# A fused LoRA kernel: ScalarE's spreads go into hardware loops, the casts to GpSimd, and the last loaded tile goes as 120 rows and 8

## The chip, the core and the metric

The kernel runs on one core of a Trainium2 chip. TensorE multiplies matrices, VectorE and ScalarE work element by element, GpSimd helps with copies, SyncE issues the transfers, and 16 DMA engines move the data between the chip's main memory and the core's own memory (SBUF). TensorE writes to PSUM.

The metric is the time of one execution on the device in microseconds (us). Three runs of the kernel before took 123.73, 123.73 and 123.92 us; the median is 123.73.

## The reference

```python
x: 16 x 512 x 768, A: 768 x 16, B: 16 x 768, all float32; scale = 0.5

def reference(x, A, B, scale):
    lora = np.matmul(np.matmul(x, A), B)
    return (x + scale * lora).astype(np.float32)
```

The output is as large as x, 25.17 MB each. Both go through the DMA engines once; A and B are small.

## The kernel before

**Tiles and parts.** x has 8192 rows of 768 numbers, 64 tiles of 128 rows. All 64 tiles have their own place in SBUF (`x_all`), and the result is added into the same place. `PARTS` cuts the 64 tiles into five parts of 8, 16, 16, 12 and 12; each partition holds neighbouring rows, so that one row of a transfer is long. Eight loads (`LOADS`) bring x in, five stores (`STORES`), one for each part, take the result out. All are issued by SyncE, in program order, on one queue.

**Groups.** The computation runs over 16 groups of four tiles (`GROUP`). A group g goes through these steps:

1. *cast* (`narrowed`, L221): four tiles of x, float32, become float16. ScalarE casts the first two tiles and GpSimd the other two.
2. *transpose* (`turned`, L277): VectorE transposes the cast group in 32 x 32 blocks into `xt`.
3. *project* (`projected`, L312): TensorE multiplies with `w_bd`, A laid out in blocks; 24 matmuls add up in PSUM (`ps_yt`).
4. *spread* (L263): ScalarE scales the product and writes it, by four instructions of 32 partitions, to the diagonal blocks of `y_bd`.
5. *raise* (`raised`, L333): TensorE multiplies with B into `lora_ps`, in two halves.
6. *add* (`summed`, L282): VectorE adds the two halves to x in place.

`xt`, the transposed group, exists once. `y_bd`, `ps_yt` and the halves of `lora_ps` exist twice. TensorE runs a hardware loop of eight rounds, each with two groups (L354): project g, raise g-1. The other engines' programs are written out at full length. VectorE's order is transpose g, then the two adds of group g-2.

**Where the cast group lies.** For groups 0 to 7 it lies in the last two of the tiles that the last load fills later (`xn_a`); for groups 8 to 10 (`PLACE`) in `xt` itself; from group 11 on in the first tiles of `x_all`, which the first store has emptied by then (`xn_c`). Each is one buffer, so the cast of a group waits until the group before it has been transposed (`s_taken`, an increment by the second matmul of each projection), in groups 8 to 10 until the projection before it is done (`s_y`), and group 11 waits for the first store (`s_out0`). VectorE's transpose waits for the projection before it, since it overwrites `xt`, and for both halves of its cast.

**SyncE's order.** The first two loads, A and B, four more loads; the seventh load once the setup's buffers in its place are free; then it waits for the adds of the first two parts and for eight projections to have begun, issues the last load, waits for the seventh load to land, and issues the stores of parts 0 and 1; the stores of parts 2 to 4 follow as their last adds finish.

**Setup.** GpSimd clears buffers, prepares `w_one` from A and copies it into three of the four diagonal blocks of `w_bd` (L247), waiting after each copy; VectorE makes the fourth copy (L292).

Of the kernel before, what the change touches and what calls it, by code (L numbers as in the profile page):

```python
# [16 lines left out]
GROUP = 4  # L17

SUB = 2
# [4 lines left out]
PLACE = range(8, 11)  # L24
# [7 lines left out]
def kernel(  # L32
# [10 lines left out]
    P = 128  # L43
# [50 lines left out]
        v = x_all[:, ds(t, SUB), :].rearrange("p s d -> p (s d)").bitcast(MM_DT)  # L94
        return v.rearrange("p (s d) -> p s d", s=GROUP)

    xn_a, xn_c = narrow_in(ROOM - SUB), narrow_in(0)

    def narrow_of(g):
        return xn_a if g < PLACE[0] else xt if g in PLACE else xn_c  # L100

    sems = []

    def sem(name):
        sems.append(nc.alloc_semaphore(name))
        return sems[-1]
# [22 lines left out]
    ]  # L129
    s_load = [sem(f"s_load{k}") for k in range(len(LOADS))]  # L130

    def load_of(t):
        i, s = where[t]
        return next(k for k, ld in enumerate(LOADS) if ld[0] == i and ld[1] <= s < ld[1] + ld[2])
# [9 lines left out]
    s_y, s_lora = sem("s_y"), sem("s_lora")  # L144
    s_spread = [sem(f"s_spread{h}") for h in range(2)]


# [13 lines left out]
    def on_sync(e):  # L161
        def load(k):
            ld = LOADS[k]
            e.dma_start(out=held(*ld), in_=memory(x2, *ld)).then_inc(s_load[k], 16)

        def summed(k):
            e.wait_ge(s_sum, k + 1)
            if STORED[k] + 1 < NG:

                e.sem_inc(s_free[STORED[k] % 2][PAIRS - 1], 1)  # L170

        def store(k, done):
            st = STORES[k]
            e.dma_start(out=memory(out2, *st), in_=held(*st)).then_inc(done, 16)
# [34 lines left out]
    def narrowed(e, copy, g, first, n=SUB):  # L209
        t = g * GROUP + first  # L210
        for k in dict.fromkeys(load_of(t + k) for k in range(n)):
            if (e, k) not in here:
                here.add((e, k))
                e.wait_ge(s_load[k], 16)
# [6 lines left out]
        ins = copy(out=narrow_of(g)[:, ds(first, n), :], in_=tiles(t, n))  # L221

        ins.then_inc(s_narrow[g % 2] if g else s_first if first else s_a, 1)

    def on_gpsimd(e):
        e.memset(a_rows[0:Q], 0.0).then_inc(s_ready, 1)  # L226
        e.memset(b_rows, 0.0).then_inc(s_brows, 1)
        e.memset(pick, 0.0).then_inc(s_pick, 1)
        e.memset(w_bd.rearrange("p c k m -> p (c k m)").bitcast(fp32), 0.0)  # L229
        e.memset(y_bd.rearrange("p h s m -> p (h s m)").bitcast(fp32), 0.0).then_inc(s_ready, 1)  # L230
        e.wait_ge(s_pick, 1)
        e.affine_select(
            out=pick, in_=pick, compare_op=mybir.AluOpType.not_equal, fill=1.0, base=0,
            pattern=[[0, NQ], [-APART, Q]], channel_multiplier=1,
        ).then_inc(s_pick, 1)
        narrowed(e, e.tensor_copy, 0, 0)
        e.wait_ge(s_pick, 2)
        e.wait_ge(s_b, 16)
        e.tensor_copy(out=b_half, in_=b_rows).then_inc(s_bh, 1)  # L239
        e.wait_ge(s_ready, 3)  # L240
        e.tensor_copy(  # L241
            out=w_one.rearrange("i (c e) k r -> i c e (k r)", c=SETS),
            in_=a_t[0:Q].rearrange("i k r (e c) -> i c e (k r)", c=SET)[:, 0:SETS, 0:SET, :],
        ).then_inc(s_w, 1)
        e.wait_ge(s_w, 1)
        for b in range(NQ - 1):
            e.tensor_copy(  # L247
                out=w_bd[ds(b * Q, Q), :, :, ds(b * Q, R)], in_=w_one
            ).then_inc(s_w, 1)
            e.wait_ge(s_w, b + 2)  # L250
        for g in range(1, NG):
            narrowed(e, e.tensor_copy, g, SUB)

    def on_scalar(e):
        narrowed(e, e.copy, 0, SUB)
        e.wait_ge(s_bp, 1)
        e.copy(out=b_mm, in_=lora[0][:, 0, :]).then_inc(s_bm, 1)  # L257
        narrowed(e, e.copy, 1, 0)
        for g in range(NG):
            e.wait_ge(s_y, g + 1)  # L260
            for b in range(NQ):
                q = ds(b * Q, Q)
                last = e.mul(out=y_bd[q, g % 2, :, q], in_=y_ps[g % 2][q, :, :], mul=sc)  # L263
            last.then_inc(s_spread[g % 2], 1)
            if g + 2 < NG:
                narrowed(e, e.copy, g + 2, 0)

    def on_vector(e):
        e.wait_ge(s_a, SETS * 16 + 1)
        e.transpose(  # L270
            out=a_t[0:Q].rearrange("i k r c -> i (k r) c"),
            in_=a_rows[0:Q].rearrange("c (i k r) -> c (k r) i", k=2, r=R),
        ).then_inc(s_ready, 1)

        def turned(g):
            ts = [v.bitcast(fp32) for v in (xt, narrow_of(g))]
            e.transpose(out=ts[0], in_=ts[1]).then_inc(s_turned[g % 2], 1)  # L277

        def summed(g, p):
            xs = tiles(g * GROUP + 2 * p, 2)  # L280
            e.wait_ge(s_lora, (g + 1) * PAIRS + p + 1)
            ins = e.tensor_tensor(out=xs, in0=xs, in1=lora[p % 2], op=mybir.AluOpType.add)  # L282
# [7 lines left out]
        b = NQ - 1  # L290
        e.wait_ge(s_w, 1)
        e.tensor_copy(  # L292
            out=w_bd[ds(b * Q, Q), :, :, ds(b * Q, R)], in_=w_one
        ).then_inc(s_wv, 1)
        for t in range(1, NG + 2):
            if t < NG:
                e.wait_ge(s_y, t)
                e.wait_ge(s_narrow[t % 2], 2 * ((t + 1) // 2))  # L298
                turned(t)
            if t > 1:  # L300
                for p in range(PAIRS):
                    summed(t - 2, p)

    def on_tensor(e):


        def projected(h):
            xv = xt.rearrange("p s (c j k) -> p s c j k", c=NC, k=2)
            e.wait_ge(s_turned[h], 1)
            for m in range(MMS):  # L310
                c, k = divmod(m, 2)
                mm = e.matmul(  # L312
                    y_ps[h], w_bd[:, c, k, :], xv[:, :, c, :, k],
                    start=(m == 0), stop=(m == MMS - 1),
                )
                if m == 0:
                    mm.then_inc(s_turned[h], -1)
                if m == 1:

                    mm.then_inc(s_taken, 1)  # L320
                if m == MMS - 1:
                    mm.then_inc(s_y, 1)

        def raised(h, p):
            if p == 0:
                e.wait_ge(s_spread[h], 1)
            free = s_free[1 - h][p]
# [12 lines left out]
            mms[-1].then_inc(s_lora, 1)  # L340
# [70 lines left out]
```

## Time and profile before

| what | value |
|---|---|
| median of three runs | 123.73 us |
| the profiled execution | 123.87 us |
| its span, first to last instruction | 122.1 us |
| DMA traffic in the span | 50.45 MB, mean 413 GB/s |
| share of the span that data packets took on 16 engines | 96.7% |
| VectorE busy | 82.8 us, 68% |
| TensorE busy (matmul, weight load) | 56.6 us, 37.0 us |
| ScalarE busy | 42.8 us, 35% |
| GpSimd busy | 30.7 us, 25% |
| instruction packets in the span (queue 14) | 2, 0.02 MB |

The profile shows one execution. PE is TensorE's matmul, PEld its weight load, DVE is VectorE, ACT is ScalarE, POOL is GpSimd, SP is SyncE, and a q behind an engine's name means its sequencer, which issues transfers. "L277" is line 277 of the kernel before. The rows of DMA and GB/s cut the span into 40 slices (a digit is the busy share in tenths, 9 is 90% or more). A row of a group reads: line, engine, operation, output<-input with shapes, count | busy us, mean ns of one | idle time before it and what ended that. A row of the timeline reads: start in us, duration in us, engine, line, operation, count, and in brackets the idle time of the engine before it and what ended it. The DMA view can be asked for any stretch of the span; it counts the packets that start in it, how many of them are small, and what share of 16 engines' time over that stretch they took, by queue: q1 carries data, q14 instructions. A packet is counted with its whole duration where it starts, so a short stretch can show more than 100%.

### The profile page before, as it was taken

How to read it: one execution, taken by the hardware profiler on the slowest of the kernel's cores; microseconds unless marked ns; L12 is line 12 of the kernel's file. 1: busy time of each engine (PE TensorE's matmuls, PEld its weight loads, DVE VectorE, ACT ScalarE, POOL GpSimd, SP SyncE). 2: the span in 40 equal slices, each digit the busy share in tenths (PEclk: the TensorE clock that was granted, in tenths of full speed). 3: DMA queues.
4: the chain of work that ended last, by engine and by line, in shares of the span. 5: the costliest groups of instructions: out<-in, count | busy, mean ns of one | idle time of the engine just before them, and what ended most of it. 6: DMA issues, size and time to landing. Idle time of an engine off the chain costs nothing.

```text
span 122.1 us, 1371 instructions
## 1 busy us (share of the span) xinstructions
PE 56.6 (46%) x522; PEld 37.0 (30%) x522; DVE 82.8 (68%) x50; ACT 42.8 (35%) x82; POOL 30.7 (25%) x31
## 2 busy tenths in 40 slices
PE   0000278775764766737694608876475740000000
PEld 0000075453351542514464208444154320000000
DVE  0002905599999999999969649999999998000000
ACT  4003344782652735265252084474380300000000
POOL 7722660441340422224040044034040000000000
PEclk9999999999999999999859995899999999655555
DMA  3999999998998989999999999799799799899980
GB/s 60 421 441 439 443 419 435 435 548 370 403 515 379 459 387 399 439 395 427 431 431 467 430 499 467 322 515 467 306 515 483 305 495 423 387 423 507 423 387 36
DMA packets 1930, 50.45 MB, mean 413 GB/s; under 512 B 236, under 2 KB 236, under 8 KB 392
## 3 DMA queue, kind: packets, MB, share of 16 engines
q1 hardware_dynamic: 1928, 50.43, 96.7%
q14 instruction: 2, 0.02, 0.0%
HBM read 25.26 MB, written 25.17 MB: 413 GB/s over the span
## 4 chain that ended last, share of the span: by engine, by line
DMA 45%; DVE 25%; issue 5%; PE 4%; POOL 4%; SPq 1%; POOLq 0%; DVEq 0%
DMA x_sb<-in_x_dram 29%; DVE x_sb L282 15%; DMA out_dram<-x_sb 9%; DVE xt L277 9%; DMA x_sb<-in_A_dram 6%; PE ps_yt L312 3%; DVE x_sb L270 2%; POOL w_bd L247 1%; POOL x_sb L221 1%; SPq L181 1%; POOL x_sb L226 1%; POOL x_sb L241 1%; PE lora_ps L333 1%; POOLq L406 0%; DVEq L298 0%
## 5 line engine op out<-in xcount | busy, mean ns | idle before, releaser
L282 DVE TENSOR_TENSOR x_sb<-x_sb,lora_ps 128x1536 f32<-128x1536 f32 x32 | 54.0, 1730 | 0.0
L312 PE MATMUL ps_yt<-xt,w_bd 128*128 128x128 f16 x384 | 27.8, 233 | 19.7 <-DVE xt L277 17.0
L333 PE MATMUL lora_ps<-b_mm,y_bd 128*128 128x512 f16 (+1 forms) x136 | 28.7, 340 | 12.2 <-DVE x_sb L282 8.6
L312 PEld LDWEIGHTS ps_yt<-xt,w_bd 128*128 128x128 f16 x384 | 25.2, 103 | 25.7 <-issue 25.7
L221 ACT CAST x_sb<-x_sb 128x1536 f16<-128x1536 f32 x13 | 19.1, 1472 | 35.9 <-PE ps_yt L312 18.9
L221 POOL CAST x_sb<-x_sb 128x1536 f16<-128x1536 f32 x13 | 19.1, 1468 | 40.3 <-PE ps_yt L312 29.2
L277 DVE STREAM_TRANSPOSE xt<-x_sb 128x1536 f32<-128x1536 f32 x13 | 22.9, 1763 | 8.3 <-POOL x_sb L221 4.8
L333 PEld LDWEIGHTS lora_ps<-b_mm,y_bd 128*128 128x128 f16 x136 | 11.8, 102 | 25.3 <-DVE x_sb L282 11.7
L263 ACT ACTIVATE y_bd<-ps_yt 32x128 f16<-32x128 f32 x64 | 17.2, 268 | 6.2 <-PE ps_yt L312 5.3
L270 DVE STREAM_TRANSPOSE x_sb<-x_sb 32x1024 f32<-32x1024 f32 x1 | 1.9, 1941 | 11.3 <-DMA x_sb<-in_A_dram 11.3
L221 ACT CAST xt<-x_sb 128x1536 f16<-128x1536 f32 x3 | 4.4, 1472 | 9.6 <-PE ps_yt L312 9.6
L221 POOL CAST xt<-x_sb 128x1536 f16<-128x1536 f32 x3 | 4.4, 1469 | 13.0 <-PE ps_yt L312 13.0
L345 PE MATMUL lora_ps<-x_sb 128*128 128x512 f16 (+1 forms) x2 | 0.8, 500 | 12.6 <-POOL x_sb L239 12.6
L277 DVE STREAM_TRANSPOSE xt<-xt 128x1536 f32<-128x1536 f32 x3 | 5.3, 1778 | 1.1 <-POOL xt L221 1.0
L345 PEld LDWEIGHTS lora_ps<-x_sb 128*128 128x128 f16 x2 | 0.1, 104 | 12.5 <-issue 12.5
L239 POOL CAST x_sb<-x_sb 128x768 f16<-128x768 f32 x1 | 0.8, 829 | 4.6 <-DMA x_sb<-in_B_dram 4.6
L221 ACT ACT_TABLE_LOAD x1 | 1.3, 1283 | 0.9 <-SPq L159 0.9
L247 POOL COPY w_bd<-x_sb 32x384 f16<-32x384 f16 x3 | 1.5, 501 | 0.2
L229 POOL MEMSET w_bd<- 128x1536 f32 x1 | 1.4, 1373 | 0.0
L257 ACT CAST b_mm<-lora_ps 128x768 f16<-128x768 f32 x1 | 0.8, 799 | 0.8 <-PE lora_ps L345 0.8
L226 POOL MEMSET x_sb<- 32x1024 f32 x1 | 0.9, 942 | 0.5 <-SPq L159 0.5
L241 POOL CAST x_sb<-x_sb 32x384 f16<-32x384 f32 x1 | 0.8, 829 | 0.9 <-DVE x_sb L270 0.9
(9 smaller groups left out, 2.6 us busy)
## 6 DMA issues: line engine op xcount, KB each, us to landing
out_dram<-x_sb SPq DMA_DIRECT2D x2, 6144.0 KB, 24.0
x_sb<-in_x_dram SPq DMA_DIRECT2D x3, 3072.0 KB, 20.7
out_dram<-x_sb SPq DMA_DIRECT2D x2, 4608.0 KB, 18.0
x_sb<-in_x_dram SPq DMA_DIRECT2D x1, 6144.0 KB, 34.8
x_sb<-in_x_dram SPq DMA_DIRECT2D x1, 4608.0 KB, 45.2
out_dram<-x_sb SPq DMA_DIRECT2D x1, 3072.0 KB, 11.4
x_sb<-in_x_dram SPq DMA_DIRECT2D x1, 2304.0 KB, 9.6
x_sb<-in_x_dram SPq DMA_DIRECT2D x1, 1536.0 KB, 9.5
```

Source lines behind the costliest of these rows:

```text
L181: e.dma_start(out=a_rows[c : SET * SET : SET, :], in_=blocks[ds(c * SET, SET), :]).then_inc(s_a, 16)
L221: ins = copy(out=narrow_of(g)[:, ds(first, n), :], in_=tiles(t, n))
L226: e.memset(a_rows[0:Q], 0.0).then_inc(s_ready, 1)
L229: e.memset(w_bd.rearrange("p c k m -> p (c k m)").bitcast(fp32), 0.0)
L241: e.tensor_copy(out=w_one.rearrange("i (c e) k r -> i c e (k r)", c=SETS), in_=a_t[0:Q].rearrange("i k r (e c) -> i c e (k r)", c=SET)[:, ...
L247: e.tensor_copy(out=w_bd[ds(b * Q, Q), :, :, ds(b * Q, R)], in_=w_one).then_inc(s_w, 1)
L263: last = e.mul(out=y_bd[q, g % 2, :, q], in_=y_ps[g % 2][q, :, :], mul=sc)
L270: e.transpose(out=a_t[0:Q].rearrange("i k r c -> i (k r) c"), in_=a_rows[0:Q].rearrange("c (i k r) -> c (k r) i", k=2, r=R),).then_inc(s_r ...
L277: e.transpose(out=ts[0], in_=ts[1]).then_inc(s_turned[g % 2], 1)
L282: ins = e.tensor_tensor(out=xs, in0=xs, in1=lora[p % 2], op=mybir.AluOpType.add)
L312: mm = e.matmul(y_ps[h], w_bd[:, c, k, :], xv[:, :, c, :, k], start=(m == 0), stop=(m == MMS - 1),)
L333: mms.append(e.matmul(t[:, k, ds(n0, w)], y_bd[:, h, 2 * p + k, :], b_mm[:, ds(n0, w)], start=True, stop=True,))
```

## The change

- *Casts.* GpSimd now casts all four tiles of a group in one instruction, except in groups 8 to 10, where ScalarE and GpSimd still share. `xn_a` and `xn_c` become two buffers each, used in turn, so that a cast waits for the transpose of the group two before (`s_taken` at g-1). In groups 8 to 10 the cast waits for `s_raise`, an increment of the first matmul of each raise, where it waited for `s_y`.
- *Spreads.* ScalarE's spreads of groups 0 to 5 and of groups 10 to 15 stand in two hardware loops of three rounds with two spreads each; those of groups 6 to 9 are written out. In loops the counts that a wait is for can't grow, so `s_y` becomes one semaphore for each of the two buffers, set to one by the projection and taken back by the second instruction of the spread.
- *Waits of VectorE.* The transpose no longer waits for `s_y`; the third instruction of the spread of the group before counts into `s_narrow`, the semaphore of the casts, and the transpose waits for one number.
- *Setup.* The fourth copy into `w_bd` moves from VectorE to ScalarE. GpSimd no longer waits after each of its three copies, but once behind them.
- *The last load.* Its four tiles go as three transfers: three tiles over 128 partitions, then the fourth tile as 120 partitions and as 8. They count into one semaphore (48 in all).

```diff
-    xn_a, xn_c = narrow_in(ROOM - SUB), narrow_in(0)
+    xn_a = [narrow_in(ROOM - GROUP + SUB * h) for h in range(2)]
+    xn_c = [narrow_in(SUB * h) for h in range(2)]
...
+    MANY = 120
+
+    def load_pieces(ld):
+        i, s, n = ld
+        if ld is not LOADS[-1]:
+            return [(held(*ld), memory(x2, *ld))]
+        three, one = (i, s, n - 1), (i, s + n - 1, 1)
+        return [(held(*three), memory(x2, *three))] + [
+            (held(*one)[rows], memory(x2, *one)[rows]) for rows in (ds(0, MANY), ds(MANY, P - MANY))
+        ]
...
-            e.dma_start(out=held(*ld), in_=memory(x2, *ld)).then_inc(s_load[k], 16)
+            for to, of in load_pieces(ld):
+                e.dma_start(out=to, in_=of).then_inc(s_load[k], 16)
...
         if g in PLACE:
-            e.wait_ge(s_y, g)
+            e.wait_ge(s_raise, g)
         elif g == PLACE[-1] + 1:
             e.wait_ge(s_out0, 16)
-        elif g:
-            e.wait_ge(s_taken, g)
+        elif g > 1:
+            e.wait_ge(s_taken, g - 1)
...
-            e.wait_ge(s_w, b + 2)
+        e.wait_ge(s_w, NQ)
         for g in range(1, NG):
-            narrowed(e, e.tensor_copy, g, SUB)
+            if g in PLACE:
+                narrowed(e, e.tensor_copy, g, SUB)
+            else:
+                narrowed(e, e.tensor_copy, g, 0, GROUP)
...
-        narrowed(e, e.copy, 1, 0)
-        for g in range(NG):
-            e.wait_ge(s_y, g + 1)
+        b = NQ - 1
+        e.wait_ge(s_w, 1)
+        e.copy(out=w_bd[ds(b * Q, Q), :, :, ds(b * Q, R)], in_=w_one).then_inc(s_wv, 1)
+
+        def spread(h):
+            e.wait_ge(s_y[h], 1)
             for b in range(NQ):
                 q = ds(b * Q, Q)
-                last = e.mul(out=y_bd[q, g % 2, :, q], in_=y_ps[g % 2][q, :, :], mul=sc)
-            last.then_inc(s_spread[g % 2], 1)
-            if g + 2 < NG:
-                narrowed(e, e.copy, g + 2, 0)
+                ins = e.mul(out=y_bd[q, h, :, q], in_=y_ps[h][q, :, :], mul=sc)
+                if b == 1:
+                    ins.then_inc(s_y[h], -1)
+                if b == 2:
+
+                    ins.then_inc(s_narrow[1 - h], 1)
+            ins.then_inc(s_spread[h], 1)
+
+        def rounds(n):
+            with e.Fori(0, n):
+                for h in range(2):
+                    spread(h)
+
+        rounds(PLACE[0] // 2 - 1)
+        spread(0)
+        for g in PLACE:
+            narrowed(e, e.copy, g, 0)
+            spread((g - 1) % 2)
+        rounds((NG - PLACE[-1]) // 2)
...
+        count = [0, 0]
         for t in range(1, NG + 2):
             if t < NG:
-                e.wait_ge(s_y, t)
-                e.wait_ge(s_narrow[t % 2], 2 * ((t + 1) // 2))
+                count[t % 2] += 3 if t in PLACE else 2
+                e.wait_ge(s_narrow[t % 2], count[t % 2])
                 turned(t)
...
                 if m == MMS - 1:
-                    mm.then_inc(s_y, 1)
+                    mm.then_inc(s_y[h], 1)
...
             if p == 0:
+                mms[0].then_inc(s_raise, 1)
                 mms[2].then_inc(s_spread[h], -1)
```

More of the change, by code (lines that the diff above doesn't have):

```diff
@@ L95, in narrow_in @@
         return v.rearrange("p (s d) -> p s d", s=GROUP)
-    xn_a, xn_c = narrow_in(ROOM - SUB), narrow_in(0)
+    xn_a = [narrow_in(ROOM - GROUP + SUB * h) for h in range(2)]
+    xn_c = [narrow_in(SUB * h) for h in range(2)]
     def narrow_of(g):
-        return xn_a if g < PLACE[0] else xt if g in PLACE else xn_c
+        return xn_a[g % 2] if g < PLACE[0] else xt if g in PLACE else xn_c[g % 2]
     sems = []
@@ L130, with landed @@
     s_load = [sem(f"s_load{k}") for k in range(len(LOADS))]
+    MANY = 120
[7 more added lines that the diff above has]
+        ]
+    def landed(k):
+        return 16 * len(load_pieces(LOADS[k]))
     def load_of(t):
@@ L143 @@
     s_turned = [sem(f"s_turned{h}") for h in range(2)]
-    s_y, s_lora = sem("s_y"), sem("s_lora")
+    s_y = [sem(f"s_y{h}") for h in range(2)]
+    s_raise, s_lora = sem("s_raise"), sem("s_lora")
     s_spread = [sem(f"s_spread{h}") for h in range(2)]
@@ L257, in on_scalar @@
         e.copy(out=b_mm, in_=lora[0][:, 0, :]).then_inc(s_bm, 1)
-        narrowed(e, e.copy, 1, 0)
-        for g in range(NG):
-            e.wait_ge(s_y, g + 1)
+        b = NQ - 1
[3 more added lines that the diff above has]
+            e.wait_ge(s_y[h], 1)
             for b in range(NQ):
                 q = ds(b * Q, Q)
-                last = e.mul(out=y_bd[q, g % 2, :, q], in_=y_ps[g % 2][q, :, :], mul=sc)
-            last.then_inc(s_spread[g % 2], 1)
-            if g + 2 < NG:
-                narrowed(e, e.copy, g + 2, 0)
+                ins = e.mul(out=y_bd[q, h, :, q], in_=y_ps[h][q, :, :], mul=sc)
[8 more added lines that the diff above has]
+                    spread(h)
+        assert PLACE[0] % 2 == 0 and len(PLACE) == 3
+        rounds(PLACE[0] // 2 - 1)
[4 more added lines that the diff above has]
+        rounds((NG - PLACE[-1]) // 2)
     def on_vector(e):
@@ L289, in on_vector @@
         turned(0)
[L290 to L294, printed above, removed]
+        count = [0, 0]
         for t in range(1, NG + 2):
             if t < NG:
-                e.wait_ge(s_y, t)
-                e.wait_ge(s_narrow[t % 2], 2 * ((t + 1) // 2))
+                count[t % 2] += 3 if t in PLACE else 2
+                e.wait_ge(s_narrow[t % 2], count[t % 2])
                 turned(t)
```

2 lines of the change are left out of this document (1 added, 1 removed).

## The prediction

> **What bounds the kernel.** I read the page first, then the DMA view of short stretches, then the timeline. The page, its groups of instructions last:
>
> ```profile
> span 122.1 us, 1371 instructions
> ...
> DMA  3999999998998989999999999799799799899980
> ...
> DMA packets 1930, 50.45 MB, mean 413 GB/s; under 512 B 236, under 2 KB 236, under 8 KB 392
> ...
> q1 hardware_dynamic: 1928, 50.43, 96.7%
> q14 instruction: 2, 0.02, 0.0%
> ...
> L282 DVE TENSOR_TENSOR x_sb<-x_sb,lora_ps 128x1536 f32<-128x1536 f32 x32 | 54.0, 1730 | 0.0
> ...
> L221 ACT CAST x_sb<-x_sb 128x1536 f16<-128x1536 f32 x13 | 19.1, 1472 | 35.9 <-PE ps_yt L312 18.9
> L221 POOL CAST x_sb<-x_sb 128x1536 f16<-128x1536 f32 x13 | 19.1, 1468 | 40.3 <-PE ps_yt L312 29.2
> ...
> L263 ACT ACTIVATE y_bd<-ps_yt 32x128 f16<-32x128 f32 x64 | 17.2, 268 | 6.2 <-PE ps_yt L312 5.3
> ```
>
> All 16 DMA engines are busy from the second slice almost to the last: 50.43 MB through q1 in 96.7% of the span. VectorE, the busiest engine, has 82.8 us of work, and its last add ends near 103 (rows below). So the end is set by the DMA engine that finishes last, and what counts is how much each engine carries. The row of q14 matters too: two instruction packets fall inside the span and go through the same engines.
>
> "Under 512 B 236" are the four-byte packets with which an engine closes its part of a transfer: 13 transfers of x and out with 16 each, B with 16, the three of A with 4 each (208 + 16 + 12). They show when each engine is done. The DMA view of seven stretches: 61.1 to 61.2 and 61.3 to 61.9 (the last load closes), 84.1 to 84.2 (the second store), 97.6 to 98.1 and 98.6 to 98.9 (the third), 119.4 to 119.85 and 120.4 to 120.7 (the last):
>
> ```profile
> DMA packets 3, 0.04 MB, mean 369 GB/s; under 512 B 1, under 2 KB 1, under 8 KB 1
> ...
> DMA packets 34, 0.42 MB, mean 696 GB/s; under 512 B 15, under 2 KB 15, under 8 KB 15
> ...
> DMA packets 2, 0.05 MB, mean 492 GB/s; under 512 B 1, under 2 KB 1, under 8 KB 1
> ...
> DMA packets 26, 0.48 MB, mean 959 GB/s; under 512 B 13, under 2 KB 13, under 8 KB 13
> ...
> DMA packets 5, 0.07 MB, mean 246 GB/s; under 512 B 3, under 2 KB 3, under 8 KB 3
> ...
> DMA packets 13, 0.00 MB, mean 0 GB/s; under 512 B 13, under 2 KB 13, under 8 KB 13
> ...
> DMA packets 3, 0.00 MB, mean 0 GB/s; under 512 B 3, under 2 KB 3, under 8 KB 3
> ```
>
> The loads close with one engine ahead and 15 behind it. In the second store one engine is late. In the third 13 have closed by 98.1 and three come after 98.6. At the end 13 are done by 119.85, and the same number, three, close after 120.4: the packet records put these at 120.41, 120.66 and 120.67. The end therefore waits some 0.84 us (120.67 less 119.83, the thirteenth) for three engines.
>
> Two of the three are late through instruction packets. The DMA view of five stretches, 67.30 to 67.35, 67.61 to 67.63, 96.34 to 96.36, 96.65 to 96.67 and 116.5 to 116.6; the last column is a share of 16 engines over the stretch:
>
> ```profile
> q14 instruction: 1, 0.01, 38.6%
> ...
> q1 hardware_dynamic: 1, 0.02, 347.8%
> ...
> q14 instruction: 1, 0.01, 96.6%
> ...
> q1 hardware_dynamic: 1, 0.05, 700.0%
> ...
> q1 hardware_dynamic: 2, 0.07, 170.5%
> ```
>
> Each instruction packet took 309 ns (38.6% of 16 x 50 ns; 96.6% of 16 x 20 ns). The data packet right behind it took 1113 ns (347.8% of 16 x 20) and 2240 ns. Without it, by the two undisturbed packets at 116.5 (170.5% of 16 x 100 ns, so 1364 ns for 36,864 B, 27.0 B/ns), they would be 909 and 1818 ns. One fetch therefore costs its engine 0.309 + 0.204 = 0.51 us, the other 0.309 + 0.422 = 0.73 us. Without them those engines close at 120.41 - 0.51 = 119.90 and 120.67 - 0.73 = 119.94.
>
> The third late engine is the one that was ahead at 61.1. Followed packet by packet it runs without a gap, but from 61 to 103 each of its packets takes 2 to 7% longer. One of them, in the DMA view of 64 to 64.03:
>
> ```profile
> q1 hardware_dynamic: 1, 0.02, 195.8%
> ```
>
> That is 940 ns (195.8% of 16 x 30 ns) for 24,576 B, against 909. It closes at 120.66.
>
> Whose fetches these are, by the timeline (start, duration, engine, line):
>
> ```profile
> 63.84 1.11 ACT L263 ACTIVATE y_bd<-ps_yt 32x128 f16<-32x128 f32 x4
> ...
> 70.14 1.47 ACT L221 CAST x_sb<-x_sb 128x1536 f16<-128x1536 f32 x1 [5.19 <-DMA out_dram<-x_sb]
> ...
> 93.39 10.04 DVE L282 TENSOR_TENSOR x_sb<-x_sb,lora_ps 128x1536 f32<-128x1536 f32 x6
> ```
>
> At 67.3 ScalarE had run 60 of its 96 recorded instructions and stood at the 61st, the cast at 70.14. At 96.35 VectorE was at its 63rd to 65th of 73, the last adds. GpSimd runs 58 in all and no fetch is seen for it. So a program is fetched on somewhere above 58 and near 60 to 64 instructions.
>
> **The change part by part.**
>
> *Shorter programs.* In the built program, without branch labels, ScalarE goes from 97 instructions to 56, VectorE from 74 to 58, GpSimd stays at 58, TensorE at 167, SyncE goes from 41 to 43. None but TensorE's is longer than the 58 that went without a fetch, and TensorE's has none in the span. I take both fetches as gone: the two engines close at 119.90 and 119.94. Bounds: nothing gained if they stay, 0.73 on one engine if they go.
>
> *The last tile as 120 and 8 rows.* Each of the 16 engines carried 8 rows of 3,072 B of it. The trace shows 128, 16 and 4 rows on 16, 16 and 4 engines, so even shares. 120 rows split evenly over 15 engines of 8 rows, at worst (of the even splits) over 8 of 15 rows. I take 15, the nearest to what is seen: one engine is spared 24,576 B, 0.91 us, and eight get one row more. Two sizes of packet, 60.31 to 60.312 and 9.945 to 9.95:
>
> ```profile
> q1 hardware_dynamic: 1, 0.01, 1453.1%
> ...
> q1 hardware_dynamic: 1, 0.00, 151.2%
> ```
>
> 12,288 B took 465 ns, one row of B, 3,072 B, 121 ns. Cutting eight packets in two costs 8 x (349 + 121 - 465) = 0.04 us (349 is three quarters of 465), and a ninth row 0.12 us. If the spared engine is the slow one, it closes at 120.66 - 0.91 + 0.04 = 119.79. The trace has no engine numbers, so I can't read that it is. But it may also matter to no timed run: it loses nothing once the last add is done (the three are as late at 98.6 as at 120.4), so it is slowed only while instructions run, and the recording of the profile may do that. I take it that it no longer sets the end. The Trainium skill ("DMA: Bandwidth & Descriptors", section "Latency and other measured facts") says that engines 7 and 15 are usually the slower ones, and in "Why a DMA increments its semaphore by 16 and not by 1" that 120 rows go to the 15 lowest engines. By these, the spared engine is the slow one if that is 15 (123.2), and the slow one gets a ninth row if it is 7 (123.9, the first rival); no row here tells which.
>
> *Sum.* The last closing is then that of the engine which lost the 0.73: 119.94 + 0.04 + 0.12 (it may be among the eight) = 120.10. Before it was 120.67, so -0.57 us. Everything behind it (1.4 us to the span's end, 1.8 us outside the span) stays.
>
> *Casts, spreads and waits.* All of this lies beside the transfers, as long as each transfer is issued before the engines run dry. The timeline of what it moves:
>
> ```profile
> 18.81 1.78 DVE L277 STREAM_TRANSPOSE xt<-x_sb 128x1536 f32<-128x1536 f32 x1 [3.43 <-PE ps_yt L312]
> ...
> 22.72 1.78 DVE L277 STREAM_TRANSPOSE xt<-x_sb 128x1536 f32<-128x1536 f32 x1 [2.13 <-POOL x_sb L221]
> ...
> 29.63 1.54 PE L312 MATMUL ps_yt<-xt,w_bd 128*128 128x128 f16 x24 [0.95 <-DVE xt L277]
> ...
> 32.71 1.76 DVE L277 STREAM_TRANSPOSE xt<-x_sb 128x1536 f32<-128x1536 f32 x1
> ...
> 63.96 1.78 DVE L277 STREAM_TRANSPOSE xt<-xt 128x1536 f32<-128x1536 f32 x1 [1.00 <-POOL xt L221]
> ...
> 70.17 1.47 POOL L221 CAST x_sb<-x_sb 128x1536 f16<-128x1536 f32 x1 [6.31 <-DMA out_dram<-x_sb]
> ...
> 71.74 1.78 DVE L277 STREAM_TRANSPOSE xt<-x_sb 128x1536 f32<-128x1536 f32 x1 [2.69 <-POOL x_sb L221]
> ...
> L292 DVE COPY w_bd<-x_sb 32x384 f16<-32x384 f16 x1 | 0.4, 446 | 0.0
> ...
> L247 POOL COPY w_bd<-x_sb 32x384 f16<-32x384 f16 x3 | 1.5, 501 | 0.2
> ```
>
> GpSimd now makes whole casts, 2 x 1.47 = 2.94 us, one group ahead, in a period of 5.0: hidden (5.0 is VectorE's 1.76 + 2 x 1.73 less overlaps). ScalarE's cast goes, so its spread starts at TensorE's end (31.17) and not at 31.50. VectorE's transpose now waits for the third spread, 3 x 0.27 = 0.8 us after TensorE's end (32.0), and is due at 32.71: 0.7 us of cover, in which the loop's branch must fit. Behind that wait stand VectorE's adds, and behind those SyncE. At the start there is no cover: group 1 slips from 18.81 by 0.8, group 2 by some 1.25 us (its release is TensorE's end plus 0.8, no longer GpSimd's cast). The fourth copy of w_bd moves to ScalarE and stays beside GpSimd's three, 0.45 to 0.50 us each, of which the last ends later: nothing. In groups 8 to 10 cast and spread stand in series and VectorE has no cover: 0.8 each, and up to 0.3 more as the cast now waits for a first matmul of 512 columns and the add that frees its PSUM buffer: VectorE is late by 1.25 + 3 x 1.1 = 4.6 us at most at group 10 (63.96 before). Group 11 waits for the first store (70.1) anyway and then for 1.47 us more of casting: 73.2 instead of 71.74, so from there it is late by 1.4, at most 2.2 us.
>
> Two transfers depend on it, by SyncE's issues:
>
> ```profile
> 0.97 0.85 SPq L164 DMA_DIRECT2D x_sb<-in_x_dram  x2
> ...
> DMA packets 4, 0.02 MB, mean 22 GB/s; under 512 B 0, under 2 KB 0, under 8 KB 4
> ...
> 52.84 0.33 SPq L164 DMA_DIRECT2D x_sb<-in_x_dram  x1
> ...
> 103.46 0.33 SPq L174 DMA_DIRECT2D out_dram<-x_sb  x1
> ```
>
> The last load is issued at 52.84 + 1.25 = 54.1, as three transfers until about 55.5; engines start to run dry at 57.4 (61.15 less eight packets of 465 ns). The last store goes from 103.46 to 104.9 (at most 105.7); 13 engines close the store before it from 108.5 on (the view of 108.5 to 109 answers with the same row as that of 97.6 to 98.1). An issue needs 1 us until its packets start (the first load is issued at 0.97, and the view of 0.9 to 2.0 holds its first four packets, from 1.98 on), so 2.6 us of cover are left, at most 1.8 are lost beyond my value. Nothing of this reaches the end.
>
> **The profiled execution** took 123.87, so 123.30; it lies 0.14 above the median of 123.73, from which I get 123.16, rounded 123.2.
>
> **The rivals.**
>
> *The slow engine stays last.* Fetches gone, but the spared engine is another, and the slowness is real in timed runs: 120.66 + 0.04, or + 0.16 with a ninth row; +0.03 to +0.15, 123.8 to 123.9. For it: the slow engine is unnumbered. Chance 0.14.
>
> *A fetch stays.* Should one program still be fetched in the span, that engine closes at 120.41 to 120.67 plus up to 0.16: 123.6 to 123.9. Against: 58 went without. Chance 0.07.
>
> *Loops that fetch again (slower).* ScalarE jumps back four times, two in each loop of three rounds. If a jump back fetched its block anew, each would cost one engine 0.51 to 0.73; four on one engine 2.0 to 2.9 us, 119.9 + 0.16 + 2.0 = 122.1 or later against 120.67: 125.2 to 126. From the second fetch on it decides. Against: TensorE's loop of eight rounds runs in the span, and q14 shows only the two packets already explained. Chance 0.06. The Trainium skill ("Runtime: NRT & Kernel Launch", section "Instruction fetch mechanics") warns that a taken branch to a target outside the current two pages forces a fetch; a loop of ten instructions in a program of 56 should stay inside, and the trace agrees as far as TensorE's loop goes.
>
> *120 rows on eight engines.* Seven rows more on each of them, then one more: 119.94 + 0.04 + 8 x 0.12 = 120.94, +0.27, 124.0. Chance 0.04.
>
> *VectorE too late.* Over 2.6 us more at group 12, each further us is one us at the end; 0.05, some 124.5.
>
> **How the numbers follow.** The forecast has 0.64. What a measurement tells from no change is about 0.2%, 0.25 us. Faster: 0.64 and a small part of the second rival, 0.66. Same: the slow engine, most of the fetch that stays, 0.20. Slower: loops, eight engines, VectorE, 0.14. The range goes from 122.9 (the thirteenth engine's 119.83 sets the end, and no engine that closes late has a ninth row) to 123.9 (the slow engine with a ninth row); what is left out is the slower part. The likeliest case alone spans 122.9 to 123.4.
>
> **What would show it.** In the profile after: no q14 row; 236 + 23 = 259 packets under 512 B (closings 16, 15 and 8 in place of 16), and 1928 + 128 + 23 = 2079 on q1; the last load's spared engine closing 0.9 us before the others; the last closings of all engines within 0.7 us, up to 120.1; casts of 2.94 us on GpSimd; the last store issued at 104.5 to 105.7. Wrong it is if an engine closes at 120.6 again, if q14 has packets, or if the share of DMA dips before 108.

## The result and the profile after

The changed kernel takes 125.31 us (median of four runs, 125.07 to 125.51), the kernel before 123.75 beside it. The ratio is 1.0122, with a 95% interval of 1.0101 to 1.0144: slower by 1.2%, where 123.2 and a gain of 0.4% were forecast.

The page of the kernel after, with the lines that answer to those of before:

```profile
span 122.8 us, 1356 instructions
...
DMA  3999999999799989998999998998999899999980
...
DMA packets 2079, 50.43 MB, mean 411 GB/s; under 512 B 259, under 2 KB 259, under 8 KB 543
...
q1 hardware_dynamic: 2079, 50.43, 96.5%
...
L323 DVE TENSOR_TENSOR x_sb<-x_sb,lora_ps 128x1536 f32<-128x1536 f32 x32 | 54.0, 1731 | 0.0
...
L240 POOL CAST x_sb<-x_sb 128x3072 f16<-128x3072 f32 (+1 forms) x13 | 34.3, 2650 | 19.6 <-PE ps_yt L350 8.8
...
L288 ACT ACTIVATE y_bd<-ps_yt 32x128 f16<-32x128 f32 x64 | 17.2, 269 | 50.1 <-PE ps_yt L350 49.0
```

The packets are those that were counted ahead: 2079 on q1, 259 under 512 B, and no q14 row, so both fetches are gone from the span. The casts, the spreads and the transposes have moved as described. Yet the span is 122.8 and not 122.1.

The DMA view of the kernel after, of 119.0 to 119.2, 119.8 to 120.9 and 121.3 to 121.6, shows the last closings ("under 512 B" counts them):

```profile
DMA packets 5, 0.15 MB, mean 737 GB/s; under 512 B 1, under 2 KB 1, under 8 KB 1
...
DMA packets 15, 0.04 MB, mean 34 GB/s; under 512 B 14, under 2 KB 14, under 8 KB 14
...
DMA packets 1, 0.00 MB, mean 0 GB/s; under 512 B 1, under 2 KB 1, under 8 KB 1
```

One engine is done at 119.08, by the packet records (the trace's list of all packets with start, duration and size, from which the DMA view counts); that is the one spared by the 120 rows. Fourteen follow between 119.90 and 120.86. The last comes alone at 121.44. Before, thirteen were done by 119.83 and the last at 120.67. So the spared engine is ahead of the fourteen by 0.8 us or more, as the prediction had it, but the fourteen are later than the thirteen were, and the last closing came 0.77 us later instead of 0.57 earlier.

That is half of the loss between the two profiled executions. The other half lies outside the span. The profiled execution of the kernel after took 125.41 against 122.8 of span, 2.6 us outside; before it was 123.87 against 122.1, 1.8 us. The DMA view behind the span's end, of the kernel before from 122.1 on:

```profile
DMA packets 0, 0.00 MB, mean 0 GB/s; under 512 B 0, under 2 KB 0, under 8 KB 0
```

and of the kernel after from 122.9 on:

```profile
DMA packets 1, 0.01 MB, mean 2 GB/s; under 512 B 0, under 2 KB 0, under 8 KB 0
...
q14 instruction: 1, 0.01, 0.8%
```

A fetch of instructions, 8,192 B in 512 ns, starts at 125.13, 2.3 us behind the last instruction. Before there was none. Last closing +0.77, the time outside the span +0.75: the two make up the 1.54 us between the profiled executions (125.41 less 123.87) to within 0.02.

### The profile page after: what moved, and what is told of

It is laid out like the page before. It is cut to its first block, busy times and chain, and to the rows that moved or that the text cites. A ratio compares the mean times of both kernels' runs of the same rounds, so it can differ in the third digit from the quotient of the medians.

```text
span 122.8 us, 1356 instructions
## 1 busy us (share of the span) xinstructions
PE 58.3 (47%) x522; PEld 36.5 (30%) x522; DVE 82.3 (67%) x49; ACT 25.7 (21%) x71; POOL 46.0 (37%) x31
## 2 busy tenths in 40 slices
DMA packets 2079, 50.43 MB, mean 411 GB/s; under 512 B 259, under 2 KB 259, under 8 KB 543
## 3 DMA queue, kind: packets, MB, share of 16 engines
q1 hardware_dynamic: 2079, 50.43, 96.5%
## 4 chain that ended last, share of the span: by engine, by line
DVE 55%; PE 11%; DMA 6%; ACT 6%; issue 3%; POOL 3%; SPq 1%; ACTq 0%; POOLq 0%
DVE x_sb L323 32%; DVE xt L318 21%; PE ps_yt L350 9%; DMA x_sb<-in_A_dram 6%; ACT y_bd L288 4%; ACT xt L240 3%; DVE x_sb L311 2%; POOL w_bd L266 1%; PE lora_ps L371 1%; SPq L200 1%; POOL x_sb L245 1%; POOL x_sb L260 1%; ACTq L297 0%; ACTq L235 0%; POOLq L445 0%
## 5 line engine op out<-in xcount | busy, mean ns | idle before, releaser
L240 POOL CAST x_sb<-x_sb 128x3072 f16<-128x3072 f32 (+1 forms) x13 | 34.3, 2650 | 19.6 <-PE ps_yt L350 8.8
L371 PE MATMUL lora_ps<-b_mm,y_bd 128*128 128x512 f16 (+1 forms) x136 | 31.1, 361 | 12.4 <-DVE x_sb L323 7.8
L350 PE MATMUL ps_yt<-xt,w_bd 128*128 128x128 f16 x384 | 27.0, 229 | 19.8 <-DVE xt L318 17.1
L350 PEld LDWEIGHTS ps_yt<-xt,w_bd 128*128 128x128 f16 x384 | 24.5, 101 | 26.7 <-issue 26.7
L240 ACT CAST x_sb<-x_sb 128x1536 f16<-128x1536 f32 x1 | 1.5, 1473 | 9.0 <-DMA x_sb<-in_x_dram 9.0
```

The source lines that it names most:

```text
L350: mm = e.matmul(y_ps[h], w_bd[:, c, k, :], xv[:, :, c, :, k], start=(m == 0), stop=(m == MMS - 1),)
L371: mms.append(e.matmul(t[:, k, ds(n0, w)], y_bd[:, h, 2 * p + k, :], b_mm[:, ds(n0, w)], start=True, stop=True,))
```

## The experiments

Two theories stood after the result. *The cut*: the three transfers in place of one make the last load, and what follows on its engines, dearer than short rows alone should. Its rivals were the changed casts and waits, and the slow engine. *The late fetch*: with fewer than some number of instructions ScalarE's program is fetched on only after the end, and the execution waits for it. Its rivals were the loops, and the shorter program of VectorE. Below, "outside" is the time of an execution less its span, and every time stands beside the kernel before on the same chip.

### The cut alone, and the rest alone

*e1* is the kernel before with nothing but the cut of the last load (in `load_pieces`, as in the change's diff, and the count of 48 that the casts wait for):

```diff
-            e.dma_start(out=held(*ld), in_=memory(x2, *ld)).then_inc(s_load[k], 16)
+            for to, of in load_pieces(ld):
+                e.dma_start(out=to, in_=of).then_inc(s_load[k], 16)
...
-                e.wait_ge(s_load[k], 16)
+                e.wait_ge(s_load[k], landed(k))
```

> The kernel before with one edit: the last load goes as three tiles, 120 rows and 8 rows. Theory S (the split costs it: packets of 3,072 B beside the first store's packets take 150 to 250 ns instead of 121): the span grows by 0.7 to 0.9 us, the part of the time outside the span stays at 1.8 us, and the time is 124.4 to 124.7; two instruction packets stay in the span. Rival C (the casts and spreads cost it, through VectorE's lateness or GpSimd's traffic): no change, 123.6 to 123.9.

Measured: 124.79 against 123.95, ratio 1.0065 [1.0041, 1.0090]; span 123.0, outside 1.81. The cut alone loses 0.84 us, all of it in the span. Both fetches are in the span here, as in the kernel before (65.84 and 97.19).

*e2* is the kernel after with the last load in one piece:

```diff
-        if ld is not LOADS[-1]:
-            return [(held(*ld), memory(x2, *ld))]
+        return [(held(*ld), memory(x2, *ld))]
```

> The changed kernel with its last load whole again. Theory S with theory F (an instruction fetch that was done in the span before now comes after it and lengthens the part outside the span from 1.8 to 2.5 us): the span goes back to 122.0 (the slow engine stays last at 120.66), the part outside stays at 2.5, 124.4 to 124.7 in all; no instruction packet in the span, one behind it. Rival C: the span stays at 122.7 or more, 125.1 to 125.4.

Measured: 124.49 against 123.95, ratio 1.0050 [1.0034, 1.0067]; span 122.05, outside 2.41. The span is that of before, and the 0.54 us lie outside it. Its last closings, by the DMA view of 119 to 120.2 and of 120.2 to 121, and behind the span from 122.1 on:

```profile
DMA packets 16, 0.04 MB, mean 31 GB/s; under 512 B 15, under 2 KB 15, under 8 KB 15
...
DMA packets 1, 0.00 MB, mean 0 GB/s; under 512 B 1, under 2 KB 1, under 8 KB 1
...
q14 instruction: 1, 0.01, 0.4%
```

Fifteen engines are done by 120.11 and the slow one, late at each closing from the last load on, comes at 120.61. So the two fetches were removed with no gain: before, the slow engine closed at 120.66 beside the two that they delayed. The last store is issued at 106.47, later than in the kernel after (105.56), and the span is none the worse: the casts and waits reach nothing at the end. The 0.84 of e1 and the 0.54 of e2 make 1.38 of the 1.56 us that the whole change lost; the 0.18 between them is no more than the intervals of the three ratios leave open.

### ScalarE's program made longer

*e3* is e2 with waits that are already met, 48 on ScalarE (24 instructions, two waits to one) and 40 on VectorE (20), so that both programs have 80 and 78 instructions. *e3a* has those of ScalarE alone.

```diff
+        for _ in range(48):
+            e.wait_ge(s_bp, 1)
...
+        for _ in range(40):
+            e.wait_ge(s_first, 1)
```

> As the run without the split, and ScalarE's and VectorE's programs made longer by 24 and 20 waits that are met already (80 and 78 instructions), placed where both engines wait anyway. Theory F: both programs pass some 64 instructions in the span, two instruction packets come back into it, the part outside falls to 1.8 us and the time to 123.7 to 123.9, what the kernel before takes. If the part outside has another cause (the branches of the loops, the semaphores): it stays at 2.5 us and the time at 124.4 to 124.8.

> As the run before this one, but only ScalarE's program is made longer. Theory F says that the part outside depends on the program whose end was not fetched in time: if VectorE's (58) is enough, it stays at 2.4 to 2.6 us with one instruction packet in the span; if it was ScalarE's alone (56), it falls to 1.8 us.

Measured: e3 123.99, ratio 1.0002 [0.9993, 1.0012], outside 1.81; e3a 123.91, 1.0001 [0.9991, 1.0011], outside 1.80. The loss of e2 is gone in both, so what was added to ScalarE's program undoes it, and VectorE's length plays no part. The DMA view of e3 from 0 to 127, the whole execution with what lies behind the span, and of e3a:

```profile
q1 hardware_dynamic: 1928, 50.43, 92.9%
q14 instruction: 2, 0.02, 0.0%
```

```profile
q1 hardware_dynamic: 1928, 50.43, 92.9%
q14 instruction: 1, 0.01, 0.0%
```

Each padded program brings its fetch back into the span (e3 at 59.36 and 72.93, e3a at 72.69), and none is left behind the end. Neither in e3 nor in e3a did a fetch within the span move the time that can be measured.

*e7* asks for the smallest cure: e2 with four such waits on ScalarE, two instructions more, 58 in all. The loops stay.

```diff
+        for _ in range(4):
+            e.wait_ge(s_bp, 1)
```

> The changed kernel with the last load whole and ScalarE's program at 58 instructions instead of 56 (four waits that are met already), the length of VectorE's and GpSimd's. Theory F with the limit between 56 and 58: no instruction packet, neither in the span nor behind it, the part outside the span 1.8 us, the span 121.9 to 122.1, the time 123.7 to 123.9. If the limit lies higher, or if the loops and not the length cause the late fetch: 2.4 to 2.6 us outside, 124.4 to 124.6.

Measured: 123.90, ratio 0.9998 [0.9988, 1.0007]; outside 1.80. The DMA view of e7 from 0 to 127:

```profile
DMA packets 1928, 50.43 MB, mean 397 GB/s; under 512 B 236, under 2 KB 236, under 8 KB 392
...
q1 hardware_dynamic: 1928, 50.43, 92.9%
```

No instruction packet at all, neither in the span nor behind it, with the loops in place. The late fetch belongs to a program of 56 and not to one of 58. (The added waits stand ahead of the loops and so move these too; no run separates the program's length from the place of its loops.) And with all fetches gone the time is that of the kernel before. The DMA view of e7 from 119 to 120.1 and from 120.1 to 122:

```profile
DMA packets 16, 0.04 MB, mean 34 GB/s; under 512 B 15, under 2 KB 15, under 8 KB 15
...
DMA packets 1, 0.00 MB, mean 0 GB/s; under 512 B 1, under 2 KB 1, under 8 KB 1
```

Fifteen engines are done by 120.04 and the slow one closes at 120.88.

### What in the cut costs the time

*e4* is the kernel after with the last load as three tiles and one, both over all 128 partitions: the short rows of 3,072 B without the 120 and 8.

```diff
-        return [(held(*three), memory(x2, *three))] + [
-            (held(*one)[rows], memory(x2, *one)[rows]) for rows in (ds(0, MANY), ds(MANY, P - MANY))
-        ]
+        return [(held(*three), memory(x2, *three)), (held(*one), memory(x2, *one))]
```

> The changed kernel with the last load as two transfers, three tiles and one tile, both over all 128 partitions. Theory S in the form that the short rows cost it: the rows of 3,072 B beside the first store's packets again take 150 to 250 ns, the first store closes 0.3 to 0.9 us later than without a split, span 122.5 to 122.9. Rival: the uneven 120 and 8 rows cost it: the span is that of the run without a split, 122.0 to 122.1. The part outside the span stays at 2.4 to 2.6 us in both.

*e5* is the opposite: the whole load in long rows of 12,288 B, cut into 120 and 8 partitions.

```diff
-        three, one = (i, s, n - 1), (i, s + n - 1, 1)
-        return [(held(*three), memory(x2, *three))] + [
-            (held(*one)[rows], memory(x2, *one)[rows]) for rows in (ds(0, MANY), ds(MANY, P - MANY))
+        return [
+            (held(*ld)[rows], memory(x2, *ld)[rows]) for rows in (ds(0, MANY), ds(MANY, P - MANY))
         ]
```

> The changed kernel with the whole last load, rows of 12,288 B, as 120 partitions and 8. Short-row theory: packets of 465 ns as without a split; one engine closes 3.7 us before the others, eight have a row more (0.46 us). If the slow engine is among those eight, it closes at 121.0 to 121.1 (span 122.4 to 122.5); if it is one of the seven others, at 120.6 (span 122.0). Uneven-rows theory: packets of 600 ns and more beside the store, span over 122.8.

*e6* makes the cut of the change on the load before the last, whose packets run at 57 to 58 us, before the first store's.

```diff
-        if ld is not LOADS[-1]:
+        if ld is not LOADS[-2]:
```

> The changed kernel with the three-way cut on the last tile of the load before the last, whose packets run at 54 to 58 us, before any store's. If it is the neighbourhood of the store's packets that makes short rows slow: rows take 121 ns, the last closings lie at most 0.2 us behind those of the run without a split, span 122.0 to 122.3. If short rows of this layout are slow by themselves: 150 to 250 ns again and a span of 122.6 to 122.9.

Measured: e4 124.59, ratio 1.0062 [1.0041, 1.0082], span 122.2, outside 2.39, so the late fetch and little else (e2's span is 122.05); e5 128.90, 1.0414 [1.0396, 1.0431], span 126.45; e6 125.92, 1.0162 [1.0138, 1.0187], span 123.35, over the range that was expected for slow rows. Rates can be read from the DMA view where a stretch holds one kind of packet: the share of q1 x 16 engines x the stretch, divided by the count. First the last load whole, the kernel before from 58.3 to 61.1:

```profile
DMA packets 99, 1.22 MB, mean 434 GB/s; under 512 B 0, under 2 KB 0, under 8 KB 0
...
q1 hardware_dynamic: 99, 1.22, 102.7%
```

99 packets of 12,288 B took 1.027 x 16 x 2.8 us, 465 ns each. The same load in e5, from 59.95 to 63.8:

```profile
DMA packets 68, 0.88 MB, mean 230 GB/s; under 512 B 0, under 2 KB 0, under 8 KB 0
...
q1 hardware_dynamic: 68, 0.88, 98.6%
```

68 packets of 12,288 B would be 0.84 MB and not 0.88: by the packet records four of them are 24,576-B rows of the first store, one behind the other on the spared engine, of 936 ns each. The other 64 took 0.986 x 16 x 3.85 us less 4 x 0.936, 890 ns each. And e4 from 60.6 to 61.0, the short rows over 128 partitions, then e6 from 57.2 to 57.8, the short rows as 120 and 8:

```profile
DMA packets 45, 0.13 MB, mean 315 GB/s; under 512 B 4, under 2 KB 4, under 8 KB 45
...
q1 hardware_dynamic: 45, 0.13, 78.1%
```

```profile
DMA packets 46, 0.14 MB, mean 236 GB/s; under 512 B 0, under 2 KB 0, under 8 KB 46
...
q1 hardware_dynamic: 46, 0.14, 96.9%
```

Four of e4's 45 packets are closings; the other 41 took 0.781 x 16 x 0.4 us, 122 ns each, the price in the prediction. In e6 it is 46 in 0.969 x 16 x 0.6 us, 202 ns each, though no store's packet is near. So neither the length of the rows nor the stores beside them is to blame. The kernel after differs from e4 in the 120 and 8 partitions alone: it is the cut along the partitions. With long rows the engines run at about half their rate, and 8 x (890 - 465) = 3.4 us of the 4.25 by which e5's span is over e4's are there. With short rows it varies along the transfer: by the packet records, the 128 of them took 177 ns on the mean in e6, 176 in the kernel after and 153 in e1, where e4's took 121. The packets behind them suffer too: in e6 the 12,288-B rows of the load that follows took 545 ns on the mean (465 undisturbed), in the kernel after the first store's 24,576-B rows 925 (914 in e4).

The 9,216-B rows of the three tiles took 368 ns on the mean in the kernel after, but 366 in e4 as well, so the 120 and 8 don't slow these. For eight rows, 366 and 121 in place of 465 are 0.18 us; e4's span shows 0.15 over e2's, no more than single runs of one kernel differ by.

### Is it the fifteen engines?

In e5 120 rows go over fifteen engines. *e8* and *e9* are e7 with the last load in long rows as 96 and 32 partitions, and as 64 and 64: the packets under 512 B are 252, 16 more than in e7, so all 16 engines take part in both halves.

```diff
+        if ld is not LOADS[-1]:
+            return [(held(*ld), memory(x2, *ld))]
+        return [
+            (held(*ld)[rows], memory(x2, *ld)[rows]) for rows in (ds(0, 96), ds(96, P - 96))
+        ]
```

(e9: `ds(0, 64), ds(64, P - 64)`.)

> The run with ScalarE at 58 instructions and the last load whole, but that load cut into 96 partitions (6 rows for each of 16 engines) and 32 (2 rows each). Theory K (it is the count of 15 engines, or the engine left out, that slows the transfer): packets of 465 ns, span 122.0 to 122.2. Theory M (any cut that gives an engine other rows than a whole transfer of 128 does slows it, since engines then meet at the same partitions): packets of 600 to 900 ns for the last load, span 123 to 126.

> The same with 64 and 64 partitions, 4 rows for each of 16 engines in both. Theory K: packets of 465 ns, span 122.0 to 122.2. Theory M: each half has 16 engines on 64 partitions, packets of 600 to 900 ns, span 123 to 126.

Measured: e8 126.95, ratio 1.0234 [1.0212, 1.0255], span 125.1; e9 127.85, 1.0316 [1.0297, 1.0334], span 126.05. The DMA view of e8 from 58.3 to 62, and of e9 from 58.6 to 60.8:

```profile
q1 hardware_dynamic: 66, 0.81, 95.3%
```

```profile
q1 hardware_dynamic: 34, 0.42, 91.8%
```

855 ns and 950 ns a packet, by the same working (0.953 x 16 x 3.7 us over 66; 0.918 x 16 x 2.2 us over 34), against 465. Fifteen engines in place of sixteen are not needed for it: every cut of the long rows by partitions that was tried costs about half the rate. Eight rows an engine at these prices are 3.1 and 3.9 us more; the spans grew by 3.0 and 3.95 over e7's 122.1.

The Trainium skill ("SBUF — State Buffer", section "Door 1: The DMA port swizzle (why `[64,N]` ≈ `[32,N]`)") says that the bandwidth of a transfer depends on how many of 16 ports its partitions reach, and that partitions 0 to 63 reach only half of them. The 950 ns of e9 agree. By the page's formula 96 and 120 partitions reach all 16 ports, so that rule by itself does not give the half rate of e8 and e5. If fifteen engines took eight neighbouring rows each and went through them in step, they would stand on half of the ports at any moment, which is worked out from the page's formula and would fit e5; the same working for 96 rows gives less of a loss than the 855 ns measured. No trace here shows ports, so for 96 and 120 partitions the cause of the half rate stays open.

### The slow engine

*e10* is e7 with 4 of the 24 matmuls of each projection.

```diff
-            for m in range(MMS):
+            for m in (0, 1, MMS - 2, MMS - 1):
```

> The run with ScalarE at 58 instructions and the last load whole, with 4 of the 24 matmuls of each projection; the other 20 are left out, so the projection is not the reference's. If the slow engine is slowed by the running of instructions (their recording), 640 instructions fewer than 1,360 halve what it loses: it closes at 119.8 to 120.3 instead of 120.6 to 120.9, its packets during the stores come near 909 ns for 24,576 B. If its slowness has nothing to do with them: 120.6 to 120.9 again.

Measured: 123.42 against 123.98, ratio 0.9954 [0.9938, 0.9971]; span 121.6. The page of e10, and its DMA view of 119 to 120.05 and of 120.05 to 121.4:

```profile
span 121.5 us, 716 instructions
```

```profile
DMA packets 15, 0.00 MB, mean 0 GB/s; under 512 B 15, under 2 KB 15, under 8 KB 15
...
DMA packets 1, 0.00 MB, mean 0 GB/s; under 512 B 1, under 2 KB 1, under 8 KB 1
```

716 recorded instructions instead of e7's 1356. The last engine now closes at 120.11, where e7's closes at 120.88, and fifteen are done by 120.05. Followed packet by packet, its stores' packets of 24,576 and 49,152 B took 930 and 1852 ns on the mean, in e7 935 and 1889, and on the other engines 912 and 1815. So with fewer instructions it loses half as much on the longer packets, and hardly less on the shorter ones, which had been expected near 909. Only matmuls were left out, so its slowness goes with how many of them run. Whether the recording of instructions, their own traffic, or something else that grows with the matmuls loads that engine is open; no run here separates these.

### The cut with the longer program

*e11* is the kernel after, cut and all, with ScalarE at 58 instructions by the four waits of e7.

> The changed kernel as it is, the cut of the last tile included, with ScalarE's program at 58 instructions (four waits that are met already). If the two causes add up and have nothing to do with each other: the part outside the span falls to 1.8 us, the span stays at 122.7 to 122.9 with the last engine closing at 121.3 to 121.5, the time is 124.5 to 124.7. If they are tied to each other, the span moves by more than 0.3 us or the part outside stays over 2.2.

Measured: 124.57 against 123.93, ratio 1.0047 [1.0029, 1.0065]; span 122.75, outside 1.81. That is 0.74 us below the kernel after, nearly all of it outside the span. In its profiled execution, the longest of the four, the spared engine closes at 119.03 and the slow one last, at 121.70, later than expected; no q14 packet is left. What remains is the cut: 0.64 us here, 0.84 in e1, which has the two fetches in its span besides.

## Why the prediction was wrong

**What bounds the kernel: right.** The end was and is set by the DMA engine that finishes last.

**Shorter programs: the fetches went, the gain didn't come.** Both left the span, as forecast. The bounds were "nothing gained if they stay, 0.73 on one engine if they go"; what was missed is a third place, behind the end. "Everything behind it (1.4 us to the span's end, 1.8 us outside the span) stays" is the step that failed: the 1.4 stayed, the 1.8 became 2.54 (e2: 2.41). The figure of 58 as a program that goes without a fetch was right, and e7 shows it for ScalarE. ScalarE was put at 56, and a shorter program was taken to be as safe. The trace of before had no program shorter than 58 but SyncE's 41, which shows nothing of the kind; so the step had no row for 56, and put the cost there at nothing without a reason. The runs show 0.54 us for it (e2).

**The last tile as 120 and 8 rows: the counts right, the price wrong.** 120 rows went to fifteen engines, one engine was spared and closed first, and the packets came to the number. "Cutting eight packets in two costs 8 x (349 + 121 - 465) = 0.04 us" failed. The 121 ns was read from one row of B, whose load has 16 rows in all, one for each engine; the 349 was worked out and not read. Both were taken for a transfer cut into 120 and 8 partitions, of which the trace had no row. In the kernel after the short rows took 176 ns on the mean and the rows of the three tiles 368, so the term is 8 x (368 + 176 - 465) = 0.63 us. Of that 0.44 is the price of the short rows in the cut; with 128 partitions the 121 holds (e4). The first store's rows add 8 x (925 - 914) = 0.09. That is near the 0.62 us by which the sixteen last closings came later on the mean (119.77 before, 120.39 after). Why the last engine of all lost 0.77 is not resolved: no row shows whether it had a ninth row.

**"I take it that it no longer sets the end": wrong.** The spared engine closed at 119.08, the slow one at 121.44: the cut spared another engine. The other reason given, that the slowness may matter to no timed run, did not hold either: e7 has no fetch and no cut, and takes 123.90 against 123.96. The first rival ("the slow engine stays last", 0.14) was right in its mechanism. It was priced at +0.03 to +0.15, since it took the price of the rows from the same step. In e2 and e7, with no cut, that engine alone undoes the gain from the fetches: it closes at 120.61 and 120.88 against 120.66 before.

**Sum.** Forecast: last closing 120.67 less 0.57, nothing else. Measured: 0.77 more, and 0.75 more outside the span. So the 2.1 us between 123.2 and 125.31 are the gain of 0.57 that didn't come (e7), the cut with 0.84 (e1) or 0.64 (e11), and the late fetch with 0.54 (e2) or 0.74 (e11). (The chances of the three slower rivals add up to 0.15, not 0.14; nothing hangs on it.)

**Casts, spreads and waits: right.** By the timeline of the kernel after (with SyncE's issues from its own stretches, 54.0 to 54.5 and 105.4 to 106):

```profile
19.61 1.78 DVE L318 STREAM_TRANSPOSE xt<-x_sb 128x1536 f32<-128x1536 f32 x1 [4.79 <-ACT y_bd L288]
...
23.98 1.78 DVE L318 STREAM_TRANSPOSE xt<-x_sb 128x1536 f32<-128x1536 f32 x1 [2.60 <-ACT y_bd L288]
...
54.10 0.81 SPq L183 DMA_DIRECT2D x_sb<-in_x_dram  x2
...
68.28 1.78 DVE L318 STREAM_TRANSPOSE xt<-xt 128x1536 f32<-128x1536 f32 x1 [1.32 <-ACT y_bd L288]
...
70.60 8.33 POOL L240 CAST x_sb<-x_sb 128x3072 f16<-128x3072 f32 x3 [3.17 <-DMA out_dram<-x_sb]
...
73.84 1.78 DVE L318 STREAM_TRANSPOSE xt<-x_sb 128x1536 f32<-128x1536 f32 x1 [0.47 <-ACT y_bd L288]
...
105.56 0.33 SPq L193 DMA_DIRECT2D out_dram<-x_sb  x1
```

Group 1 slipped by 0.80 (18.81 to 19.61; 0.8 forecast) and group 2 by 1.26 (1.25). Group 10 came at 68.28, 4.3 us later (at most 4.6 forecast), group 11 at 73.84, 2.1 later (1.4, at most 2.2). GpSimd's whole cast took 2.8 us, 8.33 over three (2.94). The last load was issued at 54.10 (54.1), the last store at 105.56 (104.9, at most 105.7). All of it stayed beside the transfers; e2's last store, issued 0.9 us later still, cost its span nothing.

**The other rivals.** Loops that fetch again: no, there is no q14 packet in the span, nor behind it in e7, with the same loops. 120 rows on eight engines: no. VectorE too late: no. A fetch that stays in the span: no; it went behind it, a case that no rival had.

## What to carry to other kernels

Cut a transfer along its rows' length, not along its partitions: with all 128 partitions, rows of a quarter of the length cost 0.15 us at most here, while 120, 96 or 64 partitions took up to twice the time for each packet, and a spared engine saves nothing when the others, or a slower one, end last. A price read from one shape of transfer is a price for that shape. When a program gets shorter, look behind the last instruction too: time less span, and the queue of instruction packets there, show what the span doesn't.

## What the runs showed of the hardware that was not expected

- A program of 56 instructions on ScalarE brought one instruction packet 2.3 us after the last instruction, and the execution ended some 0.6 to 0.75 us later (outside 2.39 to 2.54 in the kernel after, e2, e4, e5 and e6, 1.79 to 1.82 in all others). With 58 there was none, with 80 it came in the span. That the execution waits for the packet is argued from the two going together, not shown. SyncE, with 41 to 43, had none of its own that could be told apart; why ScalarE's length matters there and SyncE's doesn't is open.
- The instruction packets of the kernels before and after have 8,192 B each, one packet for each fetch in the span. The Trainium skill ("Runtime: NRT & Kernel Launch", section "Instruction fetch mechanics") speaks of refills in blocks of 16 KiB; the traces differ.
- Loops of ten instructions brought no fetch of their own.
- Packets of transfers over 120, 96 and 64 partitions took 890, 855 and 950 ns for 12,288 B on one engine, where 128 partitions took 465.
- One engine is slower than the others by some 2 to 4% while instructions run, in all kernels looked at, and by 2% (1852 ns against 1815) with 716 instructions, where it is 4% (1889) with 1356. It is not the one that 120 rows leave out.
